# Strided attention on one core: the Q loads' DRAM side described as 32 rows of 32 KiB, their SBUF side still as 128 rows of 8 KiB

## The chip, the cores and the metric

The kernel runs on 1 core of a Trainium2 chip. The metric is the device time of one execution in microseconds (us). The version before has a median of 130.83 us over 4 runs (130.78 to 130.89).

## What is computed

Eight batches of 12 heads give 96 independent attentions of 1024 queries with 64 elements each. Only every 64th key and value takes part, so each query meets 16 keys.

```python
batch, heads, seq, dim = (8, 12, 1024, 64)      # stride = 64, float32
attend_positions = np.arange(0, seq, stride)    # 16 positions
scores  = np.einsum('bhqd,bhkd->bhqk', q, k) / np.sqrt(dim)
weights = np.exp(scores - max); weights = weights / (sum + 1e-10)
result  = np.einsum('bhqk,bhkd->bhqd', weights, v)
```

Q is 96 x 1024 x 64 floats, 25.17 MB, and the result is as large. Of K and V only the 16 selected rows of each head are read.

## The kernel before, in words

**Tiles.** The 96 heads are taken in 24 groups of four (NG = 24, HG = 4). The four heads of a group lie one behind the other in DRAM, so a group of Q is one contiguous megabyte (1,048,576 bytes). load(g), lines 76 to 78, brings it into one tile qn of 128 partitions x 2048 floats with one DMA: partition p gets the p-th run of 8 KiB. Since the whole megabyte is contiguous, the runs of partitions 4r to 4r+3 lie side by side in DRAM and make 32 KiB. The pool of qn has 11 buffers (QBUFS).

**Work on a group.** transposes(g, x), lines 167 to 178, turns half a group with eight TensorE transposes (they read the upper halves of the floats as bf16) and ScalarE copies the result to qt. scores(g) multiplies with the stationary keys into PSUM, and ScalarE takes exp into w (L198). sums(g) adds up the weights on TensorE, and VectorE takes reciprocals (L211). outputs(g, c), four times a group, multiplies the weights with the values, and VectorE scales the product into out_sb (L223). store(g), lines 230 to 234, writes out_sb to DRAM with one DMA of one megabyte, as 256 runs of 4 KiB. The pool of out_sb has 9 buffers.

**Order.** It is written out by hand (manual_schedule), and every DMA is issued from SyncE (SP), on one hardware queue. SP's order is: the keys (L71), the values (L72), the first 11 loads, and then for each group its store followed by the load of 11 groups later. A store waits for the last outputs of its group; a load of the loop waits until the transposes have read the buffer that it overwrites, and stands behind the store in SP's order. The last 11 stores have no loads between them. The keys and values are gathered with 256-byte runs, 384 KB each, and prepared once, on GpSimd, TensorE, VectorE and ScalarE, before the first group.

Of the kernel before, what the change touches and what calls it, by code (L numbers as in the profile page):

```python
# [18 lines left out]
def _ap_with(ap: bass.AP, new_ap, extra_offset: int = 0) -> bass.AP:  # L19
    return dataclasses.replace(  # L20
        ap, ap=[list(p) for p in new_ap], offset=ap.offset + extra_offset
    )


# [6 lines left out]
def kernel(  # L31
# [8 lines left out]
    nc = tc.nc  # L40

    B, H, S, D = Q.shape
# [3 lines left out]
    P = 128  # L46
    HG = 4
    NG = B * H // HG
    NC = NG // 2
    SD = S * D  # L50
# [18 lines left out]
    v_raw = const.tile([P, NC, D], FP32, name="v_raw")  # L69
    kv_src = [[stride * D, P], [2 * HG * SD, NC], [1, D]]  # L70
    nc.sync.dma_start(k_raw, _ap_with(K, kv_src))  # L71
    nc.sync.dma_start(v_raw, _ap_with(V, kv_src))  # L72

    qn = {}

    def load(g):
        qn[g] = qn_pool.tile([P, 32 * D], FP32, name="qn", tag="qn")
        nc.sync.dma_start(qn[g], _ap_with(Q, [[32 * D, P], [1, 32 * D]], g * HG * SD))

    for g in range(QBUFS):  # L80
        load(g)
# [15 lines left out]
    for c in range(2):  # L97
        for a in range(2):
            for e in range(2):
                nc.gpsimd.tensor_copy(  # L100
                    out=perm_v[:, c, a, :, e], in_=id_v[:, c, :, a]
# [7 lines left out]
    for i in range(3):  # L109
# [9 lines left out]
        out=slot_i, in0=iota_p, scalar1=4, scalar2=3,  # L119
# [8 lines left out]
        out=s_sel, in0=col4, scalar1=slot_f, scalar2=None, op0=ALU.is_equal  # L128
# [3 lines left out]
        out=mask, in0=col4, scalar1=slot_f, scalar2=None, op0=ALU.is_equal  # L132
# [19 lines left out]
    for n in range(2):  # L152
        for c in range(2):
# [5 lines left out]
            for s in range(4):  # L159
                nc.vector.tensor_scalar(  # L160
                    out=v_bd[:, 6 * n : 6 * n + 6, c, s], in0=vp,
# [78 lines left out]
    for g in range(NG):  # L240
        sums(g)
        outputs(g, 0)
        outputs(g, 1)
        if g + 1 < NG:
            scores(g + 1)
        outputs(g, 2)
        if g + 2 < NG:
            transposes(g + 2, 0)
        outputs(g, 3)
        if g + 2 < NG:  # L250
            transposes(g + 2, 1)
        store(g)
        if g + QBUFS < NG:
            load(g + QBUFS)
# [35 lines left out]
```

The softmax here doesn't subtract the row's maximum and nothing guards it: scores larger than these inputs give would overflow.

## Time and profile before

| What | Value | Where it is from |
|---|---|---|
| median of 4 runs | 130.83 us | times |
| the profiled execution | 130.78 us | times |
| its span | 129.0 us | head of the page |
| bytes moved by DMA | 51.26 MB | page, part 2 |
| share of its DMA queue | 97.7% of 16 DMA engines over the span | page, part 3 |
| VectorE, ScalarE, TensorE busy | 83.7, 86.3, 71.5 us | page, part 1 |
| a Q load, a store: issue to landing | 19.6 us, 19.1 us (medians) | page, part 6 |

The span begins with the first instruction shown and ends with the last; 1.78 us of the profiled execution's 130.78 us lie outside it. A DMA is issued by an instruction on SP, whose own duration is only that of the issue. The data are then moved by 16 DMA engines in packets, each of which the trace records with its queue, its start, its duration and its size, though not with its engine. The DMA row of the page gives the mean busy share of those engines in 40 slices of the span, and the GB/s row what they moved.

### The profile page before, as it was taken

Reading aid. Unit: us, or ns where it says so; the run is one execution under the profiler, and the core shown is the slowest. Engines: PE = TensorE matmul, PEld = TensorE weight load, DVE = VectorE, ACT = ScalarE, POOL = GpSimd, SP = SyncE. Lnnn points to the kernel's source line nnn. Section 1 sums busy time; section 2 is a strip of 40 time slices with the busy share of each in tenths; the row PEclk is TensorE's granted clock in tenths of the full one; section 3 lists DMA queues with packets and bytes.
Section 4 is the critical chain, followed back from the end, with each engine's and each line's share of the span. In section 5 each row is a group of like instructions: output and inputs, shape, how many; then the busy total and the mean of one; then the engine's idle time right before and its main releaser. Section 6 shows DMA issues by size and latency. Waiting matters only on the chain.

```text
span 129.0 us, 2215 instructions
## 1 busy us (share of the span) xinstructions
PE 71.5 (55%) x880; PEld 52.2 (40%) x880; DVE 83.7 (65%) x144; ACT 86.3 (67%) x103; POOL 5.1 (4%) x23
## 2 busy tenths in 40 slices
PE   0071675995656866667866668766678666600000
PEld 0040552864445654445544456544456443300000
DVE  6229954687678777787777787777877877840000
ACT  2173294988889888899888898888898888300000
POOL 4460000000000000000000000000000000000000
PEclk9999999999999999999999999999999999755555
DMA  2999999999999999999999999999999999999991
GB/s 66 277 417 417 429 417 422 427 412 427 406 424 437 398 424 431 414 418 424 420 433 415 418 431 417 424 424 418 422 432 405 420 417 422 417 419 419 422 372 43
DMA packets 13098, 51.26 MB, mean 397 GB/s; under 512 B 3872, under 2 KB 3872, under 8 KB 10016
## 3 DMA queue, kind: packets, MB, share of 16 engines
q1 hardware_dynamic: 13088, 51.12, 97.7%
q8 instruction: 7, 0.11, 0.3%
q14 instruction: 3, 0.02, 0.0%
HBM read 25.95 MB, written 25.17 MB: 396 GB/s over the span
## 4 chain that ended last, share of the span: by engine, by line
ACT 60%; PE 13%; DVE 6%; DMA 3%; issue 3%; POOL 3%; ACTq 1%; DVEq 1%; POOLq 0%
ACT qt L178 34%; ACT w L198 26%; PE sc L186 8%; DVE v_bd L160 3%; DMA k_raw<-in_K_dram 3%; PE qt_ps L173 3%; DVE out_sb L223 1%; PE o_ps L218 1%; POOL k_dup L96 1%; POOL perm_v L100 1%; POOL v_bf L104 1%; ACTq L285 1%; PE sm L207 1%; DVEq L285 0%; PE vp L155 0%
## 5 line engine op out<-in xcount | busy, mean ns | idle before, releaser
L223 DVE TENSOR_TENSOR out_sb<-o_ps,rec 128x512 f32<-128x512 f32 x96 | 63.2, 689 | 15.2 <-PE o_ps L218 12.9
L178 ACT COPY qt<-qt_ps 128x1024 bf16<-128x1024 bf16 x48 | 46.3, 1015 | 5.4 <-PE qt_ps L173 4.7
L198 ACT ACTIVATE w<-sc 64x512 bf16<-64x512 f32 x48 | 35.3, 736 | 13.2 <-PE sc L186 12.9
L218 PE MATMUL o_ps<-v_bd,w 128*128 128x256 bf16 x192 | 34.5, 286 | 0.1
L173 PE MATMUL qt_ps<-identity,qn 128*128 128x128 bf16 x384 | 31.6, 230 | 0.2 <-ACT qt L178 0.2
L173 PEld LDWEIGHTS <-qn 128*128 128x128 bf16 x384 | 27.6, 104 | 3.8 <-issue 2.6
L186 PE MATMUL sc<-qt,k_t 128*32 128x512 bf16 x96 | 10.0, 404 | 23.9 <-ACT qt L178 23.8
L218 PEld LDWEIGHTS <-w 128*128 128x128 bf16 x192 | 14.7, 100 | 6.8 <-issue 5.8
L186 PEld LDWEIGHTS <-k_t 128*32 128x32 bf16 x96 | 4.4, 93 | 28.9 <-issue 28.8
L211 DVE RECIPROCAL rec<-sm 128x32 f32<-128x32 f32 x24 | 8.6, 358 | 9.3 <-PE sm L207 9.3
L207 PE MATMUL sm<-s_sel,w 128*128 128x4 bf16 x192 | 8.5, 166 | 6.2 <-ACT w L198 6.2
L207 PEld LDWEIGHTS <-w 128*128 128x128 bf16 x192 | 6.5, 97 | 10.6 <-ACT w L198 10.6
L160 DVE TENSOR_SCALAR v_bd<-vp,mask 128x384 bf16<-128x384 f32 x16 | 8.5, 608 | 0.1
L146 ACT CAST k_t<-kp 64x512 bf16<-64x512 f32 x6 | 3.5, 579 | 3.4 <-PE kp L140 3.4
L140 PE MATMUL kp<-perm_k,k_dup 128*128 128x128 bf16 x12 | 1.5, 312 | 6.6 <-POOL k_dup L96 6.6
L155 PE MATMUL vp<-v_bf,perm_v 128*128 128x384 bf16 x4 | 1.7, 488 | 4.6 <-DVE v_bd L160 4.1
L140 PEld LDWEIGHTS <-k_dup 128*128 128x128 bf16 x12 | 1.2, 144 | 6.6 <-POOL k_dup L96 6.6
L118 DVE TENSOR_SCALAR slot_i<-iota_p 128x1 int16<-128x1 int16 x1 | 0.2, 157 | 4.5 <-POOL iota_p L116 4.5
L146 ACT ACT_TABLE_LOAD x1 | 1.3, 1283 | 2.5 <-DVE k_t L107 2.5
L107 DVE MEMSET k_t<- 128x1536 uint32 x1 | 1.3, 1338 | 1.1 <-PEq L271 1.1
L155 PEld LDWEIGHTS <-perm_v 128*128 128x128 bf16 x4 | 0.5, 127 | 3.7 <-issue 3.7
L96 POOL CAST k_dup<-k_raw 128x768 bf16<-128x768 f32 x2 | 1.6, 827 | 2.9 <-DMA k_raw<-in_K_dram 2.9
(15 smaller groups left out, 6.0 us busy)
## 6 DMA issues: line engine op xcount, KB each, us to landing
qn<-in_Q_dram SPq DMA_DIRECT2D x24, 1024.0 KB, 19.6
out_dram<-out_sb SPq DMA_DIRECT2D x24, 1024.0 KB, 19.1
k_raw<-in_K_dram SPq DMA_DIRECT2D x1, 384.0 KB, 4.1
v_raw<-in_V_dram SPq DMA_DIRECT2D x1, 384.0 KB, 5.3
```

Source lines behind the costliest of these rows:

```text
L96: nc.gpsimd.tensor_copy(out=k_dup[:, :, e], in_=k_raw)
L140: nc.tensor.matmul(kp[:, i], lhsT=k_dup[:, 4 * n + i].rearrange("p e d -> p (e d)"), rhs=pk, start=True, stop=True,)
L146: nc.scalar.copy(k_t[h, 4 * n : 4 * n + 4, :, :, e].rearrange("p n c s k -> p (n c s) k"), kp[h].rearrange("p n c s k -> p (n c s) k"),)
L160: nc.vector.tensor_scalar(out=v_bd[:, 6 * n : 6 * n + 6, c, s], in0=vp, scalar1=mask[:, s : s + 1], scalar2=None, op0=ALU.mult,)
L173: nc.tensor.transpose(ps[:, i], _ap_with(qb, [qb.ap[0], [2, P]], extra_offset=(8 * x + i) * 2 * P + 1), identity,)
L178: nc.scalar.copy(qt[g][:, x], ps)
L186: nc.tensor.matmul(sc[32 * j : 32 * j + 32], lhsT=kt[:, 32 * j : 32 * j + 32], rhs=_ap_with(q, [q.ap[0], [P, 8], [8 * P, 2], [1, 32]], ext ...
L198: nc.scalar.activation(out=_ap_with(wa, [wa.ap[0], [P, 8], [1, 2], [2, 32]], extra_offset=64 * a), in_=sc[64 * a : 64 * a + 64].rearrange( ...
L207: nc.tensor.matmul(sm[:, :, i], lhsT=wt[g][:, i], rhs=s_sel, start=True, stop=True)
L211: nc.vector.reciprocal(rec[g], sm.rearrange("p b i e -> p b (i e)"))
L218: nc.tensor.matmul(ps[:, :, i], lhsT=wt[g][:, 2 * c + i], rhs=v_bd[:, g // 2, g % 2].rearrange("p s d -> p (s d)"), start=True, stop=True,)
L223: nc.vector.tensor_tensor(out=out_sb[g][:, :, 4 * c : 4 * c + 4], in0=ps.rearrange("p b i (e d) -> p b (i e) d", e=2), in1=rec[g][:, :, 4 ...
```

## The change

Only load(g) changes. The order of the instructions on every engine, their waits, the tiles and the bytes stay as they were. Instead of dma_start, which gets both sides of the transfer as 128 rows of 2048 floats (8 KiB), load builds the copy instruction itself, on the same SP queue, with different patterns for the two sides: the DRAM side has 32 rows of 8192 floats (32 KiB), the SBUF side has 128 partitions of 2048 floats as before. The n-th byte read is still the n-th byte written. The keys, the values and the stores keep dma_start.

```diff
+def _copy(nc, out: bass.AP, in_: bass.AP):
+
+    sides = [
+        mybir.BassSymbolicTensorAccessPattern(
+            ap=side.ap, dtype=side.dtype, bass_ap=side,
+            is_dma=True, for_custom_bir_dma=True,
+        )
+        for side in (in_, out)
+    ]
+    return nc.sync.add_instruction(
+        mybir.InstDMACopy(
+            name=nc.get_next_instruction_name(), engine=mybir.EngineType.SP,
+            ins=sides[:1], outs=sides[1:], queue="qSPDynamicHW",
+            mode="Copy",
+        )
+    )
...
     def load(g):
         qn[g] = qn_pool.tile([P, 32 * D], FP32, name="qn", tag="qn")
-        nc.sync.dma_start(qn[g], _ap_with(Q, [[32 * D, P], [1, 32 * D]], g * HG * SD))
+        _copy(
+            nc, qn[g], _ap_with(Q, [[HG * SD // 32, 32], [1, HG * SD // 32]], g * HG * SD)
+        )
```

## The prediction

> **What bounds the kernel now.** I began with the slices of the page, since they show whether one resource is full from end to end, then took the queues.
>
> ```profile
> PE   0071675995656866667866668766678666600000
> ...
> DVE  6229954687678777787777787777877877840000
> ACT  2173294988889888899888898888898888300000
> ...
> DMA  2999999999999999999999999999999999999991
> ...
> q1 hardware_dynamic: 13088, 51.12, 97.7%
> q8 instruction: 7, 0.11, 0.3%
> ```
>
> The DMA row stands at 9 from the second slice to the last but one, while the three compute engines have gaps and are done five slices (16 us) earlier. The page's chain of work that ended last names ScalarE for 60%; it runs back from the last instruction of an engine, at 113.7 us, and doesn't see the transfers that run on to the end. So I checked the end in SP's row of time and SP's waits:
>
> ```profile
> 82.64 32.04 SPq L231 DMA_DIRECT2D out_dram<-out_sb  x11
> ```
>
> ```profile
> SPq L285 <- DMA out_dram<-out_sb: 13.3, 1, 13.3
> ```
>
> The last store is issued at 114.3 to 114.7 us, and then SP waits 13.3 us for stores to land. With a megabyte each and 420 GB/s (2.5 us), that is a backlog of several stores. The end is the end of a queue of bytes, not of the computation. The last check is the table by stretches (columns: stretch and length, busy us and instructions of PE, PEld, DVE, ACT, POOL, then the clock, the DMA share, the GB/s):
>
> ```profile
> 18.00:25.00 7.00, 5.07 (x44) 3.18 (x42) 3.00 (x6) 5.04 (x7) 0.00 (x0) 1.00 1.01 419
> ...
> 50.00:80.00 30.00, 20.84 (x287) 15.74 (x287) 22.66 (x39) 25.82 (x31) 0.00 (x0) 1.00 1.02 422
> ...
> 112.00:121.00 9.00, 1.06 (x5) 0.26 (x2) 2.27 (x4) 0.00 (x0) 0.00 (x0) 0.50 1.02 420
> ```
>
> Loads alone (18 to 25 us), loads and stores mixed, and stores alone (from 112 us) all move 419 to 422 GB/s. What a Q load costs the 16 engines is therefore paid in full by the end, one to one; nothing else in the change can matter unless it starves those engines.
>
> **What is removed: three of four reads.** Each load has 128 reads of 8 KiB and 128 writes of 8 KiB now, and will have 32 reads of 32 KiB and 128 writes of 8 KiB. Spread over 16 engines and 24 loads, an engine has 24 x 32 / 16 = 48 wide reads in place of 192 narrow ones. The bytes per engine are the same. What can be saved is a cost per packet, so I looked for one in two stretches of the DMA view, loads alone from 14 to 25 us and stores alone from 112 to 121 us:
>
> ```profile
> DMA packets 628, 4.62 MB, mean 420 GB/s; under 512 B 64, under 2 KB 64, under 8 KB 64
> ...
> q1 hardware_dynamic: 628, 4.62, 100.7%
> ```
>
> ```profile
> DMA packets 980, 3.78 MB, mean 420 GB/s; under 512 B 57, under 2 KB 57, under 8 KB 980
> ...
> q1 hardware_dynamic: 980, 3.78, 102.4%
> ```
>
> Loads: 100.7% of 16 engines x 11 us is 177.2 us, and less 64 packets of 4 bytes (under 10 ns each) it is shared by 564 packets of 8 KiB: 313 ns each. Stores: 102.4% of 16 x 9 us is 147.5 us for 923 packets of 4 KiB: 159 ns each. Two packets of 4 KiB thus take 318 ns where one of 8 KiB takes 313, so a packet has a fixed 5 ns beside some 154 ns for 4 KiB. I checked that on the single packet records between 60 and 100 us, lined up so that each starts where one before it ends: on an engine an 8 KiB packet starts 305.8 ns before its successor, a 4 KiB packet 155.3 ns, and 2 x 155.3 - 305.8 = 4.8 ns. Four narrow reads made one lose three fixed parts: 3 x 5 = 15 ns, and 48 x 15 ns = **0.72 us** for each engine. It is hidden by nothing, and no cover is needed, as the engines are busy throughout.
>
> The bounds. The 3072 packets of 256 B (keys and values) take 21 ns on average in the records, of which 154 x 256 / 4096 = 10 ns is for the bytes: 11 ns fixed, and 48 x 3 x 11 ns = 1.6 us is the most. The least gain is zero: the two stretches above have the same 420 GB/s though one has packets half as large, and no row of this profile separates the read side from the write side, whose 128 pieces stay. If the 5 ns belong to the write of a piece, or if each side has its own and they run side by side, nothing is gained. I take 0.72 us, since the steadiest rows (5 and 4.8 ns) give it. Below zero is the third rival.
>
> The Trainium skill, DMA: Bandwidth & Descriptors, "Why small descriptors are slow (HBM only)", has a fixed overhead of about 3 cycles per packet inside a DMA engine, 3.5 ns by the 850 MHz that the page gives for the fabric; by it the sum would be 48 x 3 x 3.5 ns = 0.5 us, an estimate from that page. The same section speaks against this change: it calls joining descriptors into packets worth it only up to 256 B, and 8 KiB is 32 times that; by that rule the sum would be about zero. The rows above have 5 ns of 306 left to gain, so they agree that it is small and not that it is nothing.
>
> **What is moved or added elsewhere.** No instruction moves on any engine, no wait is added, and the same buffers come free in the same order. SP's issue is written differently, so its duration may change: 24 loads take it 0.33 to 2.2 us each now, 0.44 in the median. Were each to take twice that, SP would spend 10.6 us more in all, behind its waits for VectorE's last outputs alone, which sum to 43 us, and with 19.6 us from issue to landing, so with some eight megabytes queued. The thinnest cover is at the start: the first Q load is issued at 1.98 us, and the engines move keys and values until about 5.4 us, when the first 8 KiB packets of Q start; an issue 0.4 us later is hidden, and one over 3 us later would be paid in full. I cost it at nothing, with 0.4 us as what it would be uncovered.
>
> Faster loads don't run into another wait. The 11 first loads and the keys and values are 12.3 MB, at 420 GB/s some 29 us of work from about 4 us on; the first store comes at 25.08 us, so the queue holds 8 us of work at that point, far over the 0.3 us that eleven faster loads take from it. At the end, the computation is ahead by the 13.3 us that SP waits. The engine that would come next is ScalarE, at 3.94 us a group in the chain of waits, against 5.0 us of transfer for two megabytes.
>
> **Sum.** 130.78 us of the profiled execution (129.0 of span, 1.78 around it) less 0.72 is 130.06. It stands 0.05 under the median of 130.83, so the median goes to **130.1**.
>
> **Rivals.**
> 1. The reads run faster and the fixed part goes (the forecast): 130.1, from 129.2 (all of 1.6 us) to 130.5. For it speaks that packets of 4 and of 8 KiB differ by 5 ns in the two ways of reading the records. Chance 0.57.
> 2. Nothing changes, because the fixed part belongs to the writes, or because the hardware cuts the wide read at the edges of the writes again: 130.8. For it speaks the equal 420 GB/s of both kinds. Chance 0.22.
> 3. Slower: a wide read doesn't stream as four narrow ones do. The nearest row for packets over 8 KiB is q8, instruction fetches of 16 KiB: 0.3% of 16 x 129 us is 6.2 us for 7 of them, 0.88 us each, against 2 x 0.313 = 0.63 us for the same bytes in Q packets: 0.25 us more. They share their engine with Q's packets, so that is an upper end. At 0.25 us for each of 48 wide reads it would be 12 us, 142.8 less the 0.7 saved, 142.1; with a sixth of that price, 40 ns, 132.0. It decides from 20 ns a read on: 15 ns pay back the saving, and 0.26 us / 48 = 5 ns more make it measurable. Against it speaks that packets of twice the size cost nothing more per byte between 4 and 8 KiB. If the 32 rows were dealt to the engines in such a way that two write to the same place at a time, the price would be of this kind too. Chance 0.21.
>
> The Trainium skill, same page, "The descriptor swizzle", has each engine write two blocks of four neighbouring partitions; four partitions are just one 32 KiB read, so by it each engine keeps its bytes. No row of this profile names an engine, so none shows it.
>
> **How the numbers follow.** A run to run difference of 0.2% (0.26 us) is about what can be told from no change here. Faster 0.57, same 0.22, slower 0.21. The first two cases hold 0.79; with a little of the third the range reaches from 129.2, the largest saving, to 132.0, where a wide read costs 40 ns more.
>
> **What would show it.** Right: the GB/s of 14 to 25 us up by 5/313 = 1% or more (to 425), the stores' stretch still at 420, and the end of the DMA row 0.7 us earlier with SP's last wait shorter by about as much; if the records follow reads, 768 packets of 32 KiB at about 1235 ns in place of 3072. Rival 2: the same rate in every stretch. Rival 3: a load stretch well under 415 GB/s, and PE or VectorE waiting for Q. I would be wrong in kind if SP's issues grew so long that the DMA row shows gaps, or if DMA were no longer at 9 where it is now.

## The result, and the profile after

The changed kernel has a median of 130.66 us (34 runs, 130.57 to 130.97), the kernel before 130.85 us in the same comparison (55 runs). The ratio is 0.9985, with a 95% interval of 0.998 to 0.999: 0.19 us less, where 0.72 us had been forecast.

The profiled execution took 130.87 us with a span of 129.0, so it is one of the longer ones, and its end is no shorter than that of before (130.78 us). It serves to see what became of the packets. From its page:

```profile
DMA  2999989999799999899999999999998999999981
...
DMA packets 10794, 51.26 MB, mean 397 GB/s; under 512 B 3872, under 2 KB 3872, under 8 KB 10016
...
q1 hardware_dynamic: 10784, 51.12, 97.1%
```

There are 2304 packets fewer (13098 less 10794): the 3072 packets of 8 KiB are now 768 of 32 KiB, so the packet records follow the read side. The bytes are the same, and the row is still full from end to end. In the packet records the 768 take 1238.6 ns on average.

The DMA view of the loads that run alone, 14 to 25 us, and of the stores that run alone, 112 to 121 us:

```profile
DMA packets 206, 4.65 MB, mean 423 GB/s; under 512 B 64, under 2 KB 64, under 8 KB 64
...
q1 hardware_dynamic: 206, 4.65, 100.6%
```

```profile
DMA packets 978, 3.78 MB, mean 420 GB/s; under 512 B 56, under 2 KB 56, under 8 KB 978
...
q1 hardware_dynamic: 978, 3.78, 102.5%
```

The view counts a packet's bytes where it starts, so with packets of 32 KiB a short window is off by some per cent at its edges (423 for 420 here). What the edges don't touch is the busy time of a packet: 100.6% of 16 engines x 11 us, less 64 marks (packets of 4 bytes, under 10 ns each), over 142 packets is 1243 ns, that is 311 ns for each 8 KiB. Before it was 313 by the same working: these loads have gained next to nothing. The stores are unchanged, as they should be.

The table by stretches shows the same trap, with its loads alone at 440, the mixed stretch at 426 (422 before) and the stores at 420:

```profile
18.00:25.00 7.00, 4.45 (x50) 2.94 (x49) 3.09 (x6) 5.04 (x7) 0.00 (x0) 0.76 1.05 440
...
50.00:80.00 30.00, 20.84 (x287) 15.74 (x287) 22.66 (x39) 25.77 (x31) 0.00 (x0) 1.00 1.02 426
...
112.00:121.00 9.00, 0.38 (x3) 0.10 (x1) 2.30 (x4) 0.00 (x0) 0.00 (x0) 0.56 1.02 420
```

The computation keeps its busy times to a few hundredths of a us in the mixed stretch; only the GB/s move.

SP's end of the story, from its row of time and its waits, and SP's issue of a load from the view of the tile qn (shortest, median and longest in ns):

```profile
82.45 32.25 SPq L251 DMA_DIRECT2D out_dram<-out_sb  x11
```

```profile
SPq L305 <- DMA out_dram<-out_sb: 13.2, 1, 13.2
```

```profile
L34 SPq DMA_DIRECT2D qn<-in_Q_dram x24: 471/472/2201, 2.0 to 80.0; - x24
```

The last wait is 13.2 us where it was 13.3, not 0.7 shorter. The issue is 0.03 us longer in the median, and no engine waits longer for it: the view of qn has 4.7 us of waiting by ACT in both kernels.

**Where the time went, by bytes.** To see each stretch without the blur at the edges of a window, I spread the bytes of each packet over its duration and took the time at which a given megabyte had been moved. The table has the us from one mark to the next; two profiles of three of the kernels are shown (the runs of the later rows are told below).

| Kernel | 3 to 11 MB, loads alone | 11 to 13 MB, first stores begin | 13 to 44 MB, mixed | 44 to 50 MB, stores alone |
|---|---|---|---|---|
| before | 19.04, 19.06 | 4.75, 4.75 | 73.85, 73.83 | 14.35, 14.34 |
| changed | 19.03, 19.00 | 4.89, 5.25 | 73.53, 73.47 | 14.33, 14.34 |
| only the first 11 loads changed | 19.00 | 4.90 | 73.83 | 14.33 |
| only the 13 loads of the loop changed | 19.04, 19.05 | 4.74, 4.75 | 73.60, 73.54 | 14.34, 14.33 |

The gain of 0.31 to 0.37 us is in the mixed stretch alone. The loads that run alone gain nothing, and where the first stores begin 0.14 to 0.50 us are lost. In the mixed stretch (60 to 98 us) an 8 KiB packet started 305.8 ns before its successor on an engine, and a 32 KiB packet starts 1209 ns before it: 14 ns less than four narrow ones, as forecast. While loads run alone it is 1237 to 1240 ns, four times the 309.5 ns of before.

### The profile page after: what moved, and what is told of

It is laid out like the page before. It is cut to its first block, busy times and chain, and to the rows that moved or that the text cites. A ratio compares the mean times of both kernels' runs of the same rounds, so it can differ in the third digit from the quotient of the medians.

```text
span 129.0 us, 2215 instructions
## 1 busy us (share of the span) xinstructions
PE 69.3 (54%) x880; PEld 51.1 (40%) x880; DVE 83.8 (65%) x144; ACT 86.2 (67%) x103; POOL 5.1 (4%) x23
## 2 busy tenths in 40 slices
DMA packets 10794, 51.26 MB, mean 397 GB/s; under 512 B 3872, under 2 KB 3872, under 8 KB 10016
## 4 chain that ended last, share of the span: by engine, by line
ACT 60%; PE 12%; DVE 6%; DMA 3%; POOL 3%; issue 2%; ACTq 1%; DVEq 0%; POOLq 0%
ACT qt L198 34%; ACT w L218 26%; PE sc L206 8%; DMA k_raw<-in_K_dram 3%; DVE v_bd L180 3%; PE qt_ps L193 2%; DVE out_sb L243 2%; PE o_ps L238 2%; POOL k_dup L116 1%; POOL perm_v L120 1%; POOL v_bf L124 1%; ACTq L305 1%; PE sm L227 1%; DVEq L305 0%; PE vp L175 0%
## 5 line engine op out<-in xcount | busy, mean ns | idle before, releaser
L218 ACT ACTIVATE w<-sc 64x512 bf16<-64x512 f32 x48 | 35.3, 736 | 13.2 <-PE sc L206 12.9
L238 PE MATMUL o_ps<-v_bd,w 128*128 128x256 bf16 x192 | 33.4, 278 | 0.6 <-DVE out_sb L243 0.6
L193 PE MATMUL qt_ps<-identity,qn 128*128 128x128 bf16 x384 | 30.7, 227 | 0.2 <-ACT qt L198 0.2
L193 PEld LDWEIGHTS <-qn 128*128 128x128 bf16 x384 | 27.0, 102 | 3.8 <-issue 2.6
```

The costliest lines, as they stand in the source:

```text
L193: nc.tensor.transpose(ps[:, i], _ap_with(qb, [qb.ap[0], [2, P]], extra_offset=(8 * x + i) * 2 * P + 1), identity,)
L218: nc.scalar.activation(out=_ap_with(wa, [wa.ap[0], [P, 8], [1, 2], [2, 32]], extra_offset=64 * a), in_=sc[64 * a : 64 * a + 64].rearrange( ...
L238: nc.tensor.matmul(ps[:, :, i], lhsT=wt[g][:, 2 * c + i], rhs=v_bd[:, g // 2, g % 2].rearrange("p s d -> p (s d)"), start=True, stop=True,)
```

## The experiments

Theory A, in the texts below, is my explanation after the result: the fixed part of a read shows only where stores run beside the loads. Rival B: it is saved everywhere, and lost again elsewhere.

**Only the first 11 loads, only the 13 of the loop.**

```diff
     def load(g):
-        _copy(...)
+        if g < QBUFS:            # the other kernel: if g >= QBUFS
+            _copy(...)
+        else:
+            nc.sync.dma_start(...)   # 128 rows of 8 KiB on both sides
```

> Only the first 11 loads read 32 KiB rows; the 13 loads in the loop are as before. Theory A (a packet's fixed part of about 5 ns shows only where loads and stores are mixed, since in the profile of the changed kernel a 32 KiB read there takes 1209 ns against 4 x 305.8 before, while the loads that run alone take 1237 to 1240 against 4 x 309.5): the median stays within 0.1 us of before. Rival B (every wide read saves 14 ns, and some 0.5 us are lost elsewhere, at the start or in the longer issue): 22 x 14 ns = 0.31 us less, or, if the loss sits in these first loads, up to 0.2 us more. The load-only stretch shows 1237 to 1240 ns by A, about 1224 by B.

> Only the 13 loads in the loop read 32 KiB rows; the first 11 are as before. Theory A: all of the gain is here, 26 wide reads an engine x 14 ns = 0.36 us less than before, so at least as fast as the changed kernel, and about 0.1 to 0.2 us faster than it if the first wide loads cost something at the start. Rival B, loss in the first loads: the same 0.36 us. Rival C (the longer issue of the self-built copy costs time in the loop): about 0.2 us less than before, like the changed kernel, or nothing.

With the first 11 changed: ratio 0.9999 (0.9989 to 1.0009), no change. With the 13 of the loop: 0.9989 (0.9979 to 0.9999), 0.14 us less, as much as the whole change within the intervals. 22 of the 48 wide reads of an engine thus bring nothing, and rival B's 0.31 us for them is out. Of the 0.36 us expected for the loop the table has 0.24 and 0.30 in the mixed stretch, and the end of the kernel has 0.14: see the late engine below.

**The form of the instruction without the size.**

```diff
-            nc, qn[g], _ap_with(Q, [[HG * SD // 32, 32], [1, HG * SD // 32]], g * HG * SD)
+            nc, qn[g], _ap_with(Q, [[32 * D, P], [1, 32 * D]], g * HG * SD)
```

> All 24 loads are issued with the self-built copy, but with 128 rows of 8 KiB on both sides, as before. It isolates the other form of the instruction from the size of the reads. By theory A and B: SP's issue at about 0.47 us instead of 0.44, the time within 0.1 us of before. Rival C: slower than before by 0.1 to 0.2 us, which is the part of the 0.4 us gain in the loop that the changed kernel doesn't show.

0.9999 (0.9989 to 1.0008): the self-built copy by itself costs nothing that can be told.

**The same idea on the stores.** The SBUF side of a store is read in 8 KiB pieces, and its DRAM side is written in 4 KiB pieces as before.

```diff
     def store(g):
-        nc.sync.dma_start(
+        o = out_sb[g].rearrange("p b i x -> p (b i x)")
+        _copy(nc,
             _ap_with(out, [[16 * D, P], [2 * SD, 2], [1, 16 * D]], g * HG * SD),
-            out_sb[g].rearrange("p b i x -> p b (i x)"),
+            _ap_with(o, [o.ap[0], [32 * D, 1], [1, 32 * D]]),
         )
```

> Loads as before (8 KiB on both sides). The stores are issued with the same self-built copy: their SBUF side is 128 reads of 8 KiB, their DRAM side 256 writes of 4 KiB as before. If the fixed part of about 5 ns goes with the read packet whatever memory is read: 24 stores x 8 reads fewer an engine x 4.8 ns = 0.92 us less, about 129.9, in the mixed stretch and in the stores alone (two 4 KiB packets at 310.6 ns become one of 8 KiB at 306). If it goes with reads of DRAM only, or with the write: no change in time, 310 ns for each 8 KiB.

0.9975 (0.9964 to 0.9987): 0.31 us less, with the loads as before. Its DMA view from 112 to 121 us:

```profile
DMA packets 527, 3.83 MB, mean 425 GB/s; under 512 B 60, under 2 KB 60, under 8 KB 60
...
q1 hardware_dynamic: 527, 3.83, 101.4%
```

425 GB/s where the stores alone had 420: two reads of 4 KiB made one save about 4 ns here too (306.8 ns from packet to packet, against 2 x 155.3). So the fixed part goes with the read packet, of SBUF as of DRAM, and the number of writes doesn't hide it in this stretch. Again only part of the 0.92 us arrives. By bytes the mixed stretch is 0.44 us shorter than before (73.40) and the stores alone 0.17 us (14.17); where the first stores begin, some packets take 0.5 to 0.85 us, and the stretch is 0.10 us longer (4.85).

**Do writes have a price?** Loads with 2 KiB pieces on both sides, with 8 KiB reads and 2 KiB writes, and, since these writes did not start at multiples of 256 bytes, with 8 KiB reads and two writes of 4 KiB that do. Gaps in the tile keep the pieces apart, and the transposes read from the shifted places. The diff is of the version with two writes of 4 KiB; the change in the transposes is left out of it.

```diff
-        qn[g] = qn_pool.tile([P, 32 * D], FP32, name="qn", tag="qn")
-        _copy(nc, qn[g], _ap_with(Q, [[HG * SD // 32, 32], [1, HG * SD // 32]], g * HG * SD))
+        qn[g] = qn_pool.tile([P, 2 * 1056], FP32, name="qn", tag="qn")
+        q = qn[g]
+        _copy(
+            nc, _ap_with(q, [q.ap[0], [1088, 2], [1, 1024]]),
+            _ap_with(Q, [[32 * D, P], [32 * D, 1], [1, 32 * D]], g * HG * SD),
+        )
```

> All 24 loads move 2 KiB pieces on both sides (the tile has a gap of 16 floats after each 512, so that the pieces can't be joined). Three more packets in each 8 KiB. Theory A (some 4.7 ns for each read packet, hidden in the load-only stretch up to a limit of 420 GB/s): 13 loads x 8 x 3 x 4.7 ns = 1.5 us where loads and stores are mixed, and in the 11 first loads 8 KiB go from 309.5 ns to 301 + 4 x 4.7 = 320 ns, 0.9 us: 2.4 us more than before, 133.2. If the load-only limit hid all of it: 1.5 us more. If the cost went with neither side: no change.

> All 24 loads read 8 KiB rows as before and write 2 KiB pieces (same tile with gaps), so only the number of writes is four times that of before. Theory A, the cost goes with the read: within 0.15 us of before. Rival D, the write has its own cost of the same kind: 1.5 to 2.4 us more, as in the kernel with 2 KiB on both sides. In between, by the share that the write has.

> All 24 loads read 8 KiB rows and write two pieces of 4 KiB (a gap of 64 floats between them, each piece starts at a multiple of 256 bytes, which the 2 KiB pieces of the earlier kernel did not). It asks again whether a write has a cost of its own. If only the read counts: 306 ns for 8 KiB in the mixed stretch, and the time of before within 0.15 us. If the dearer side counts (two writes beside one read): 311 ns, 13 loads x 8 x 5 ns = 0.5 us more than before.

2 KiB on both sides: 1.0213 (1.0194 to 1.0231), 133.65 us. 8 KiB reads with 2 KiB writes: 1.0206 (1.0187 to 1.0226), 133.58 us, the same with a quarter of the reads. Two writes of 4 KiB: 1.0089 (1.007 to 1.0109), 132.03 us. These are 2.8, 2.7 and 1.2 us more than before, each above what I had expected of it. My theory A in its first form falls here: writes do have a price. The DMA view of 10 to 30 us, loads alone, of the kernel before, then of those with two writes of 4 KiB, with 8 KiB reads and 2 KiB writes, and with 2 KiB on both sides:

```profile
DMA packets 1152, 8.40 MB, mean 420 GB/s; under 512 B 128, under 2 KB 128, under 8 KB 128
```

```profile
DMA packets 1123, 8.17 MB, mean 408 GB/s; under 512 B 127, under 2 KB 127, under 8 KB 127
```

```profile
DMA packets 1098, 7.96 MB, mean 398 GB/s; under 512 B 127, under 2 KB 127, under 8 KB 127
```

```profile
DMA packets 4003, 7.95 MB, mean 398 GB/s; under 512 B 126, under 2 KB 126, under 8 KB 4002
```

In the first three the reads are the same 8 KiB, and the rate falls from 420 to 408 GB/s with two writes (320 ns from packet to packet for 309.5) and to 398 with four (329 ns). In the last there are four times as many reads, and the rate stays at 398: by bytes, 3 to 11 MB take 20.15 us with 8 KiB reads and 20.16 with 2 KiB reads, for 19.04 before. Taking 301 ns for the bytes (four times 301 and 5 make the 1209 of a wide read), the fixed part in this stretch is 8 ns for one write, 9 for each of two, 7 for each of four: while loads run alone it goes with the pieces written. In the mixed stretch both sides count: 13 to 44 MB take 74.91 us with 8 KiB reads and 2 KiB writes and 75.36 with 2 KiB on both sides, for 73.84 before.

**What holds loads that run alone?** Two kernels with loads and nothing else: one with four forms of load one after the other, and one with tiles of 32 KiB a partition, in which some written pieces are as long as the reads. The diff is of the second.

```diff
+    for g in range(10):
+        narrow(g)                  # 8 KiB read, 8 KiB written
+    for g in range(12, 24, 4):
+        nc.sync.dma_start(         # 32 KiB read, 32 KiB written
+            big[g // 4 % 3], _ap_with(Q, [[128 * D, P], [1, 128 * D]], g * HG * SD))
+    for g in range(10, 18):
+        wide(g)                    # 32 KiB read, 8 KiB written
+    for g in range(6):
+        narrow(g + 18)
```

> Leaves out all of the attention: 8 loads of 8 KiB rows on 128 partitions, 8 of 32 KiB rows, then the same two on 88 partitions (11 of the 16 engines by count of rows), and one store. It asks what holds loads that run alone to 309.5 ns an 8 KiB. If it is a limit that the engines share: 309.5 ns for 8 KiB and 1238 for 32 KiB on 128 partitions, and with 11 engines 306 and 1209 (294 to 298 GB/s). If it is a limit of each engine: the same 309.5 and 1238 on 88 partitions too (291 GB/s). If it was the start of the kernel (keys, values, computation beside it): 306 and 1209 in the first 16 loads too, 426 and 432 GB/s.

> Leaves out all of the attention: loads only. 10 loads of 8 KiB rows on both sides, 3 loads of 4 MB with 32 KiB rows on both sides (tiles of 32 KiB a partition), 8 loads with 32 KiB reads and 8 KiB writes, 6 loads of 8 KiB again, one store. Explanation F (where loads run alone, each written piece costs 7 to 9 ns, and the change leaves the 128 pieces of a load as they are): 1209 to 1214 ns for a 32 KiB packet with a 32 KiB write, 1237 to 1242 with four 8 KiB writes. Explanation G (16 engines loading together share a limit of 422 GB/s, whatever the pieces): 1237 to 1242 ns for both.

The first of the two told little of its question: on 88 partitions something else bound it, as the last section tells. On 128 partitions its narrow loads moved 427 GB/s until about 16 us, then 422 to 424, and the wide ones after them 422. The second decides. Its DMA view, from 30 to 54 us (32 KiB written) and from 59 to 74 us (8 KiB written):

```profile
DMA packets 345, 10.26 MB, mean 427 GB/s; under 512 B 32, under 2 KB 32, under 8 KB 32
...
q1 hardware_dynamic: 345, 10.26, 99.3%
```

```profile
DMA packets 294, 6.39 MB, mean 426 GB/s; under 512 B 99, under 2 KB 99, under 8 KB 99
...
q1 hardware_dynamic: 294, 6.39, 101.4%
```

The edges blur the GB/s again, and the busy time of a packet doesn't: less the marks, 99.3% of 16 x 24 us over 313 packets is 1217 ns, 101.4% of 16 x 15 us over 195 is 1243 ns. A record runs some 4 ns past the start of the next packet, so from start to start it is about 1213 and 1239, as F expects. By bytes spread over durations it is 431 to 432 against 422 GB/s. The reads are alike in size (a transfer of 4 MB spreads them otherwise over DRAM, which no run varies by itself), and the row above with four times the reads at the same rate says the same: the limit of the loads that run alone is the written piece (F), and no common limit of 422 GB/s (G). The change leaves the 128 written pieces of a load as they are. The narrow loads at the end, from 78 us on, move 422 GB/s like the wide ones before them.

> Leaves out all of the attention: 11 loads of 8 KiB rows by 16 engines as before, then 13 small loads of 4 x 8 KiB to each of 8 partitions that lie 12 apart, meant to use 8 engines. If loads that run alone are held to 309.5 ns an 8 KiB by a limit that all engines share: 306 ns with eight engines. If the limit is each engine's: 309.5 ns still.

With eight engines 73% of the 8 KiB packets took 309 ns or less, the duration of the 306 ns step, where of the last three loads by sixteen 28% did and 72% took 310 to 321. This points to a cost that shows when all sixteen load at once. It doesn't prove it: 16% of the eight engines' packets took longer, up to 1.7 us, and these transfers are small, start often and write to other places.

**Loads and stores without the attention.** 24 loads and 24 stores of a constant tile take turns; the pair differs in the form of the load only.

```diff
+    for g in range(NG):
+        narrow(g)                  # the other kernel: wide(g)
+        store(g)
```

> Leaves out all of the attention: only the 24 loads, with 8 KiB rows as before, and 24 stores of a constant tile, taking turns from the start. It is the pair of the next kernel. No load runs alone for long, no keys or values, hardly any instructions to fetch. By the packets (8 x 306 + 16 x 155.3 + two marks of 6 ns = 4945 ns for a load and a store) 24 turns take 118.7 us and with the start and the end some 123 us.

> The same with 32 KiB reads in all 24 loads. Theory A (the saving is whole wherever stores run beside the loads, and only the load-only stretch hides it): 48 x 14 ns = 0.67 us less than its pair with 8 KiB rows. Rival E (the mixed stretch gives back more than half of it too, by stalls or by one late engine): 0.2 to 0.35 us less. No saving at all would speak against the 1209 ns read from the trace.

126.90 us (126.48 to 127.14 in 5 runs) and 126.32 us (125.14 to 126.77 in 6): 0.58 us less, of the 0.67 expected, but the two overlap. The line of the page on what was moved, narrow and then wide:

```profile
HBM read 25.17 MB, written 25.17 MB: 402 GB/s over the span
```

```profile
HBM read 25.17 MB, written 25.17 MB: 408 GB/s over the span
```

402 to 408 overstates it (the wide profile is of an execution of 125.14 us, its kernel's shortest). By the completion marks of the last store, one from each engine, the mean engine ends at 122.87 and 122.25 us: 0.62 us. By bytes, 10 to 20, 20 to 30 and 30 to 40 MB take 23.63, 23.57 and 23.58 us with narrow reads and 23.47, 23.45 and 23.46 with wide ones, so the saving is steady. When stores run beside all the loads, nearly all of it comes, and the stretch itself gives nothing like half of it back, as rival E had it; what a late engine takes at the end, these few runs can't tell. My 123 us for the narrow kernel fit the mean engine alone: the last ends 1.68 us behind it, and the rest lies after the last store.

**What is lost where the first stores begin.** Second profiles of the kernels:

> The changed kernel once more, for a second profile. If the loss of some 0.15 us in the stretch of 30 to 36 us, where the first stores begin, belongs to the wide first loads, it moves about 411 GB/s there again; if it was chance, about 420 as before. In 60 to 98 us: 423 GB/s again.

> The kernel before once more, for a second profile. 420 GB/s in 30 to 36 us if the stretch's rate goes with the form of the first loads, 411 to 420 if it is chance. In 60 to 98 us: 421 GB/s again.

> The kernel with wide reads in the loop alone once more, for a second profile. If the loss goes with wide first loads: no packet over 1.5 us around 32 us and 420 GB/s in 30 to 36 us; 423 GB/s in 60 to 98 us.

The table above has them (the GB/s of so short a stretch are blurred by its edges: 400 and 368 with all loads changed, 467 and 464 with those of the loop). In the changed kernel 5 packets that start at 32 us, among the last of the first 11 loads, take 1.6 to 1.9 us; in its second profile it is 23 packets around the same time, of up to 2.6 us. What they take over 1.26 us makes 0.14 and 0.48 us for each of 16 engines. With only the first 11 loads changed it is 0.15; before, and with only the loop changed, 0.01 or less in two profiles each. So the loss goes with the wide first loads, though not with them alone: with 8 KiB first loads the stretch from 11 to 13 MB takes 4.80 us in the kernel with the self-built copy and 4.85 in the one with wide reads in the stores, for 4.75 before. Why these packets wait is not settled: no view shows what a packet waits for.

**Loads and stores together.** The changed kernel with the stores of above, and the same with the first 11 loads as before:

> The changed kernel's 32 KiB reads and the stores with 128 reads of 8 KiB from SBUF. Theory A: the two savings are of different packets and add up, 0.19 us (measured for the change) + 0.31 us (measured for the stores) = 0.5 us less than before, about 130.35; in the mixed stretch a megabyte of loads plus one of stores takes 2 x 1209 + 8 x 306 + two marks an engine, 426 GB/s. If some other limit (the 420 GB/s of the load-only stretch) bounds the mixed stretch too: no faster than the stores alone, 130.55.

> The first 11 loads with 8 KiB rows as before, the 13 loads in the loop with 32 KiB reads, the stores with 8 KiB reads. If the loss at 32 us belongs to wide reads in flight when the first stores begin (32 KiB packets of 1.5 to 2.6 us in place of 1.24 there in both profiles of the changed kernel, 0.14 and 0.48 us when shared by 16 engines), this version keeps what the kernel with both changes has (0.53 us less than before) and gains another 0.1 to 0.3 us: 130.0 to 130.2. If not, it is as fast as that one, 130.3.

0.9958 (0.9944 to 0.9971), 130.31 us, and 0.9966 (0.9952 to 0.998), 130.40 us. The savings of loads and stores add up to 0.53 us as expected. Leaving the first loads alone brought no more, though the stretch lost no time there: my 0.1 to 0.3 us are not to be seen. With both kinds of wide reads a 32 KiB packet takes 1222 and 1224 ns on average from 60 to 98 us, 1215 to 1217 in the kernels with wide loads alone, which takes a part of the saving.

**The late engine.** In the kernel before, the 16 completion marks of the last store lie 2.9 us apart, from 1.03 us ahead of their mean to 1.85 behind it. The kernel ends with the last. Some single engines fall behind by about 1.2 us from 26 us on, at times when 16 KiB instruction fetches (q8) run. That the fetches are the cause is not shown: in the kernel of loads and stores with 8 KiB reads, whose trace has no fetch, the last engine is 1.68 us behind too (0.29 with 32 KiB reads). With only the loop changed the mean engine ends 0.16 to 0.32 us earlier than in the two profiles of before, but its last one is 2.21 and 2.26 us behind the mean (1.85 and 1.90 before) and ends no earlier. Whether that is chance is open; two profiles each can't tell.

## Why the prediction was right or wrong

The direction was right and the time lies in the range; the size is a quarter of the forecast, and under the 0.2% that I called a difference. So the likeliest case was the wrong one by my own bounds: 130.66 is above the 129.2 to 130.5 that I gave it. That the time lies in the whole range says little, since the range held the case of no change as well.

**What bounds the kernel** held: the DMA row is full, and what a packet gains in the mixed stretch is in the table by bytes one to one. That it is "paid in full by the end, one to one" didn't hold: the last of 16 engines ends the kernel, and with only the loop changed it ended no earlier, while the mean engine did by 0.16 to 0.32 us.

**The fixed part** of 5 ns was right where it was measured from packet to packet, between 60 and 100 us. 1209 ns for a wide read against 4 x 305.8 gives 14 ns, and 26 of them are 0.36 us; the table by bytes has 0.31 and 0.37.

The first of the two ways that gave 5 ns was no check on the second. It divides busy time by packets, and each record runs some 4 ns into the next, as the shares over 100% show. Two records of 4 KiB hold two such overlaps and one of 8 KiB holds one, so 4 of the 5 ns were overlap. From start to start the same two stretches give 2 x 155.3 - 309.5 = 1 ns. That the two ways agreed was luck.

**The step that failed** is "48 x 15 ns = 0.72 us for each engine", taken over all 48 wide reads. 22 of them belong to loads that run alone, and there each written piece of 8 KiB costs 8 ns and sets the pace, whatever the reads are: 0.33 of the 0.72 us could not come, and with the first 11 loads alone changed nothing came (0.9999). The view had said so. I quoted 420 GB/s for loads in 8 KiB packets and 420 for stores in 4 KiB packets, called the equality a lower bound, and then mixed the two stretches to get 5 ns. In the loads' stretch a step of 309.5 ns is within 1 ns of twice the 155.3 ns of the stores' packets, with almost no fixed part of the read left to save.

**Rival 2** named the mechanism, a cost on the side of the writes, as all or nothing. It holds for the first 11 loads and fails for the other 13.

**Rival 3** had the right kind of event at a small size: wide packets that stall, at one place, 0.14 to 0.50 us where the first stores begin. The rival had it in every read.

**The covers** held: SP's issue went from 0.44 to 0.47 us with no one waiting longer, and the copy with 8 KiB rows costs nothing that can be told.

Together: 0.72 forecast, less 0.33 that the writes hide, leaves 0.39; the table has 0.31 to 0.37 of it in the mixed stretch, and 0.19 was measured at the end. Where the remaining 0.2 us go is open. The loss of 0.14 us and more at the first stores would fill most of it, but the two kernels without this loss are no faster than the like ones with it: 0.14 us less than before against 0.19, and 130.40 us against 130.31.

The Trainium skill, DMA: Bandwidth & Descriptors, "Why small descriptors are slow (HBM only)", gives about 3 cycles a packet and calls joining worth it only up to 256 B. The runs have 4 to 5 ns for a read of 8 KiB or of 4 KiB where reads set the pace, near the 3.5 ns estimated from that page, so the cost is there far above 256 B; what is worth having of it was 0.15% here, and 0.4% with the stores.

## What to carry to other kernels

In these runs a fixed cost per packet had two sides, read and write, and only the side that was dearer in a stretch could be saved there: before counting packets, ask in each stretch (loads alone, mixed, stores alone) whether the rate follows the size of the reads or of the writes. Two stretches with equal rates and unequal packets are evidence against the saving there, not the lower end of a range. A saving on all engines is paid at the end only if the last of them gains it too. Measure a packet's cost from start to start on one engine within the stretch where it is to be saved.

## What the runs showed of the hardware

Loads of 88 partitions were far slower than expected: in the kernel with loads only, 8 KiB packets took 600 ns in the median where 128 partitions took 309, and 32 KiB packets 2155 ns for 1240. Its table by stretches, with narrow loads of 128 partitions from 8 us on and of 88 from 50 us on:

```profile
8.00:16.00 8.00, 0.00 (x0) 0.00 (x0) 1.00 1.01 425
...
50.00:74.00 24.00, 0.00 (x0) 0.00 (x0) 1.00 0.69 162
```

The rate falls to 162 GB/s, while 88 partitions are 11/16 of 128, and 11/16 of 425 would be 292. The share of 0.69 fits 11 of 16 engines at work, so it is the packets that are slower. Why is open.

In kernels that do nothing else, 8 KiB loads move 426 to 428 GB/s for some 16 us and then 422, without any change in the program; in the kernel with 32 KiB written the rate rose to 431 after that. In the kernel before, a packet of the first loads takes 312 ns instead of 309 from about 7 us on. So the dearer written piece needs something more than sixteen engines loading, and what that is stays open.
